# Matmuls that read the two halves of their moving operand by turns, in a two-layer transformer kernel

## The chip, the cores and the metric

The kernel runs on one NeuronCore of one Trainium2 chip, in a single launch. The metric is the device time of that core in microseconds (us), as the median of several runs. Engines are called as the profile calls them: PE (TensorE matmul), PEld (TensorE weight load), DVE (VectorE), ACT (ScalarE), POOL (GpSimd) and SP (SyncE, which issues the DMAs).

## The reference, cut to what matters

Sequence 1024, width 1024, two layers, all float32. Layer 0 mixes by sliding-window attention, layer 1 by a gated recurrence; both are followed by an MLP with a squared ReLU.

```python
for layer in range(DEPTH):                       # DEPTH = 2
    h = rmsnorm(x, mix_norm[layer])
    if layer % 2 == 0:
        y = sliding_window_attention(h, positions, attn_w_qkv[j], attn_b_qkv[j], attn_sinks[j], attn_w_o[j])
    else:
        y = hgrn2_recurrence(h, lbs[layer], hgrn_w_in[j], hgrn_g_norm[j], hgrn_w_o[j])
    x = x + y
    h = rmsnorm(x, mlp_norm[layer])
    x = x + jnp.square(jax.nn.relu(h @ mlp_w_up[layer])) @ mlp_w_down[layer]   # 1024 -> 4096 -> 1024
return rmsnorm(x, final_norm)
...
# attention: 16 query heads of 64 in 4 groups, each group with one key and value head;
# a query block of 128 sees its own and the previous block of keys, 256 in all
scores = jnp.einsum('bnqkgd,bnskd->bnkgqs', qb, kb) * (HEAD_DIM ** -0.5)
```

## The kernel before, in words

Activations lie with features on the 128 partitions and tokens along the free dimension, in two halves of 512 tokens (`TH`). So a product of a weight block and an activation is a matmul with the weights (128x128) stationary and the 512 tokens moving; in the query, key and value projection it is the other way round, 128 tokens stationary and 512 columns of weights moving. The result of each matmul fills one PSUM bank of 512 columns; there are four banks with tag `p` and four with tag `q`.

Float32 products are made from three matmuls in the format float32r. Each operand is split into a high part (a cast to float32r) and a low part (the rest); `mm3` multiplies high by high, high by low and low by high into the same bank. The splits are the bulk of the work on DVE and ACT: `weight_split` and `split` make a cast (on ACT or DVE) and a subtraction (DVE).

The large products use a two-by-two scheme with seven products in place of eight (Strassen's, in Winograd's order). `product` makes one of these: 4 blocks by 3 matmuls, 12 matmuls of 512 columns. The stages, in order of time, and their float32r matmuls of 512 columns:

- attention: the projection `qkv` (two halves, 3 column groups, 8 blocks, 4 token blocks, 3 matmuls: 576) and the output projection `o_proj` (2 by 8 by 8 by 3: 384), so 960. Between them, `attend_block` makes the scores of a query block: for four heads a matmul of 256 columns (the previous and the own block of 128 keys) with the keys' high part and one with their low part, 256 matmuls of 256 columns in all. The bank is then read in two parts: the own block's columns by a copy on ACT, the previous block's by a predicated copy on DVE.
- the MLP up projection `pair`: 16 pairs of row blocks, 7 products of 12 matmuls, 1344 in each layer. A product's bank is read by a copy on ACT or by an addition on DVE.
- the MLP down projection `down`: passes (1, 5), (6), (7), (4), (2), (3) over 16 blocks, each pass with 4 row blocks and 3 matmuls per product, 1344 in each layer. In the last layer, the last 96 of these are cut into 192 of half the width (256 columns: first tokens 0 to 255, then 256 to 511), so that the final norm and the stores of the first 256 tokens begin earlier: 1248 of 512 columns remain. `final` writes these with four DMAs for each half.
- the recurrence: `gates` and `two` make the projections of layer 1 (8 heads, 2 by 7 products, 12 matmuls: 1344), and `recurrence` the small float32 matmuls of the scan. In those, six levels of the scan use a moving operand of 32 columns out of a chunk of 64: at the first level every other column, at the last level 32 columns in a row.
- `hgrn_out`, the output projection of layer 1: 384.

Plain float32 matmuls (not float32r) remain in `spread` (512 columns), in the transposes (128 columns) and in the recurrence.

All operations are first recorded and then ordered by `Schedule.order`, a list scheduler: it plays the program with an estimated cost for every operation (the `cost` in `mm`, `act`, `copy`, `tt`, ...), fixed latencies between engines and a fixed number of buffers per tag, and issues each engine's instructions in the order that comes out. SP's queue holds the DMAs in that order too. Some operations may go to ACT or DVE (`ways`), and the scheduler chooses. So a changed cost in `mm` changes the order of all engines. Since every operation is recorded by one helper, the profile gives line 326 for nearly all of them, and groups are told apart by tile names: `a`, `t`, `m` are SBUF buffers, `wr` raw weights, `wh` and `wl` their high and low parts, `d` a buffer in DRAM.

Of the kernel before, what the change touches and what calls it, by code (L numbers as in the profile page):

```python
# [276 lines left out]

class Net:
# [153 lines left out]
    def sum_squares(self, tiles, n=TH):  # L432
        acc = None
        for x in tiles:
            sq = self.t()[:, :n]
            self.act(sq, x, AF.Square, n)
# [123 lines left out]

    def product(self, ps, w, x, start, n=TH):
# [19 lines left out]
    def pair(self, m, x):  # L581
# [3 lines left out]
        def read(ps):  # L585
            z = self.t()
            self.copy(z, ps)
            return z
# [13 lines left out]
        self.tt("DVE", u1, own, u1, ALU.add)  # L602
        self.square_relu(m, 0, u1, False)
        self.tt("DVE", u2, side, u2, ALU.add)
# [56 lines left out]
    def down(self, cut):  # L661
# [9 lines left out]
        def products(names, ps, ws, start, stop, tokens=slice(0, TH), ms=range(HK)):  # L671
            for p in ps:
                for name in names:
                    (wh, wl), (xh, xl) = ws[name, p]
                    for m in ms:
                        out = (main if name in (1, 6, 7, 4) else side)[m][:, tokens]
# [3 lines left out]
                        self.mm3(out, (wh[:, c], wl[:, c]), (xh[:, tokens], xl[:, tokens]), first, p == stop,  # L680
                                 tokens.stop - tokens.start, **more)
# [12 lines left out]
        def scaled_sum(hf, out, z, tokens=slice(0, TH)):  # L694

            k = tokens.stop - tokens.start
            u = self.t(tag="m")[:, :k]
            self.tt("DVE", u, z, self.r[hf][:, tokens], ALU.mult, k)
            part = out[:, tokens].only(tokens.start)
# [8 lines left out]
        for m in range(HK):  # L708
            y[0, 0, m], y[1, 1, m] = self.a(), self.a()
            self.copy(y[0, 0, m], main[m])  # L710
        for m in range(HK):
            self.copy(y[1, 1, m], side[m])
        run_pass((6,))
        for m in range(HK):
            u = y[0, 1, m] = self.a()
            self.copy(u, main[m])
# [4 lines left out]
        for m in range(HK):  # L721
            self.copy(parts[m], main[m])
# [14 lines left out]
        for m in range(HK):  # L737
            self.copy(parts[m], side[m])
# [17 lines left out]
        for c in (0, TH // 2):  # L756
            tokens = slice(c, c + TH // 2)
            for m in range(HK):
                products((3,), range(n - held, n), ws, False, n - 1, tokens, [m])
                scaled_sum(1, self.x[m][1], side[m][:, tokens], tokens)  # L760
            yield 1, tokens
# [100 lines left out]
    def keys_values(self, n, ps, r):  # L862
        W = NG * HD
        k = self.t(F32, (P, W))
        self.stt(k, ps[:, :W], r, self.bias[0][:, :W], ALU.mult, ALU.add, W)
# [3 lines left out]
        self.stt(v, ps[:, W:], r, self.bias[0][:, W:], ALU.mult, ALU.add, W)  # L869
# [61 lines left out]
    def attend_block(self, g, n, stacks):  # L931
# [7 lines left out]
        for h in range(4):  # L939
            self.mm(scores[h // 2][:, h % 2], stacks[h][:, tok], ks[:, c], h % 2 == 0, False, 2 * P)  # L940
        for h in range(4):
            self.mm(scores[h // 2][:, h % 2], stacks[h][:, tok], kl[:, c], False, h % 2 == 1, 2 * P)
# [29 lines left out]
    def o_proj(self, hf, out):  # L972

        a = [self.split(out[g, j]) for g in range(NG) for j in range(2)]
        for m in range(KT):
# [7 lines left out]
            self.tt("DVE", self.x[m][hf], ps, x, ALU.add)  # L983
# [62 lines left out]
    def two_first(self, which, e, x):  # L1046
# [6 lines left out]
        self.copy(y0, main)  # L1053
        self.product(own, w[1], x[2], True)
        self.tt("DVE", y0, own, y0, ALU.add)
        return main, y0

    def two(self, which, e, x, out, begun=None):
# [6 lines left out]
        if not begun:  # L1065
            self.product(main, w[1], x[1], True)
            self.copy(y0, main)
        yield
        self.product(side, w[5], x[5], True)
        self.copy(z1, side)  # L1070
        yield
        self.product(main, w[6], x[6], False)
        self.copy(y1, main)
        yield
        if not begun:
            self.product(own, w[2], x[2], True)
            self.tt("DVE", y0, own, y0, ALU.add)
        yield
        self.product(main, w[7], x[7], False)
        self.tt("DVE", z1, main, z1, ALU.add)  # L1080
        yield
        self.product(side, w[3], x[3], False)
        self.tt("DVE", y1, side, y1, ALU.add)
# [291 lines left out]
```

## Time and profile before

| what | value |
|---|---|
| median of 3 runs | 2181.03 us (2179.08 to 2183.65) |
| span of the profiled execution, first to last instruction | 2174.9 us |
| instructions | 32278 |
| PE busy | 2129.5 us (98%), 11374 matmul records |
| PEld busy | 1713.3 us (79%) |
| DVE busy | 1823.6 us (84%) |
| ACT busy | 837.7 us (39%) |
| POOL busy | 62.4 us (3%) |
| DMA | 316.49 MB, mean 146 GB/s, 44.7% of 16 engines' time |

The profile holds one execution, whose own time is known as its span alone: 2174.9 us, 6.1 us below the median of the runs. A matmul record lasts longer than the distance to the next one, since matmuls are pipelined; so the pace of the PE is read from start to start, or from a chain piece of many matmuls divided by their number. "Clock" is the share of full speed that the throttle granted.

### The profile page before, as it was taken

What the parts mean: (1) busy time and instruction counts of PE and PEld (TensorE: products, weight loads), DVE (VectorE), ACT (ScalarE), POOL (GpSimd) and SP (SyncE); (2) the same over time, 40 slices, a digit from 0 to 9 for tenths busy, and PEclk for the clock granted to TensorE, in tenths of its full rate; (3) what the DMA queues carried; (4) which work ended last, traced back from release to release, by engine and by line L of the source; (5) the groups of instructions that cost most, each with busy time, mean ns of one, the idle gap of its engine ahead of it and who ended that gap; (6) DMA issues with size and microseconds to landing.
All of it is one profiled execution on the core that took longest, in us unless ns stands there. A gap on an engine that the chain in (4) does not pass through costs nothing.

```text
span 2174.9 us, 32278 instructions
## 1 busy us (share of the span) xinstructions
PE 2129.5 (98%) x11374; PEld 1713.3 (79%) x11374; DVE 1823.6 (84%) x3608; ACT 837.7 (39%) x1757; POOL 62.4 (3%) x124
## 2 busy tenths in 40 slices
PE   8999999999999999999999999999999999999997
PEld 6777778888877887877788888878788887888786
DVE  8899889667789888899888888878976678988887
ACT  5567755122234233365333333343521223322442
POOL 4030000000000000000100000000000000000000
PEclk9999999999999999999999999999999999999999
DMA  6212363333369867741111111547333336976652
GB/s 204 75 48 83 112 194 116 105 109 111 108 204 305 274 202 234 247 136 49 56 57 59 58 53 52 188 148 227 113 114 103 107 116 224 305 241 226 209 171 78
DMA packets 174274, 316.49 MB, mean 146 GB/s; under 512 B 19616, under 2 KB 21664, under 8 KB 174112
## 3 DMA queue, kind: packets, MB, share of 16 engines
q1 hardware_dynamic: 174112, 314.43, 44.7%
q8 instruction: 89, 1.46, 0.3%
q14 instruction: 73, 0.60, 0.1%
HBM read 250.39 MB, written 63.96 MB: 145 GB/s over the span
## 4 chain that ended last, share of the span: by engine, by line
PE 85%; DVE 7%; ACT 4%; DMA 2%; issue 1%; SPq 0%; DVEq 0%; ACTq 0%
PE q L326 45%; PE p L326 40%; DVE a L326 3%; DVE t L326 2%; ACT t L326 1%; ACT a L326 1%; DVE wl L326 1%; DVE m L326 1%; DMA wr<-in_down 1%; ACT m L326 1%; ACT wh L326 0%; DMA t<-d 0%; DVE wh L326 0%; DMA d<-t 0%; DMA a<-d 0%
## 5 line engine op out<-in xcount | busy, mean ns | idle before, releaser
L326 PE MATMUL q<-a,wh 128*128 128x512 f32 x2560 | 798.6, 395 | 5.0 <-DVE t L326 2.3
L326 PE MATMUL p<-a,wh 128*128 128x512 f32 x2336 | 754.4, 402 | 9.1 <-ACT t L326 3.7
L326 PEld LDWEIGHTS q<-a,wh 128*128 128x128 f32 x2560 | 480.1, 188 | 120.5 <-ACT t L326 4.1
L326 PEld LDWEIGHTS p<-a,wh 128*128 128x128 f32 x2336 | 432.0, 189 | 107.7 <-ACT t L326 4.6
L326 PE MATMUL q<-a,wl 128*128 128x512 f32 x1280 | 499.5, 394 | 0.0
L326 PE MATMUL p<-a,wl 128*128 128x512 f32 x1168 | 462.8, 397 | 0.0
L326 PEld LDWEIGHTS q<-a,wl 128*128 128x128 f32 x1280 | 240.4, 188 | 56.6
L326 PEld LDWEIGHTS p<-a,wl 128*128 128x128 f32 x1168 | 220.4, 189 | 50.5 <-issue 0.5
L326 DVE TENSOR_TENSOR wl<-wr,wh 128x512 fp32r<-128x512 f32 x352 | 241.0, 686 | 15.5 <-ACT wh L326 5.4
L326 ACT COPY t<-q 128x512 f32<-128x512 f32 (+2 forms) x201 | 111.8, 562 | 349.0 <-PE q L326 344.1
L326 DVE TENSOR_TENSOR a<-t,a 128x512 fp32r<-128x512 f32 (+1 forms) x294 | 195.0, 685 | 0.8 <-DMA t<-d 0.5
L326 DVE CAST wh<-wr 128x512 fp32r<-128x512 f32 x204 | 87.8, 430 | 127.6 <-PE p L326 78.4
L326 DVE TENSOR_TENSOR wl<-m,wh 128x512 fp32r<-128x512 f32 x256 | 176.3, 689 | 16.1 <-ACT wh L326 6.1
L326 ACT CAST wh<-m 128x512 fp32r<-128x512 f32 x153 | 95.2, 623 | 210.4 <-PE q L326 148.4
L326 DVE TENSOR_TENSOR t<-t,t 128x512 f32<-128x512 f32 (+3 forms) x268 | 159.7, 611 | 17.7 <-DMA t<-d 10.7
L326 ACT CAST a<-t 128x512 fp32r<-128x512 f32 x189 | 114.7, 619 | 128.8 <-PE q L326 82.6
L326 ACT CAST wh<-wr 128x512 fp32r<-128x512 f32 x148 | 91.1, 619 | 172.7 <-PE p L326 109.3
L326 PE MATMUL p<-wh,a 128*128 128x512 f32 x384 | 130.6, 407 | 8.2 <-ACT a L326 7.0
L326 DVE TENSOR_TENSOR m<-wr,wr 128x512 f32<-128x512 f32 x160 | 109.7, 687 | 22.2 <-DMA wr<-in_down 11.9
L326 PEld LDWEIGHTS q<-t,t 128*64 128x64 f32 (+1 forms) x2160 | 98.0, 144 | 25.0 <-issue 11.2
L326 PE MATMUL q<-t,t 128*64 128x32 f32 (+2 forms) x2160 | 111.5, 230 | 0.0
L326 DVE CAST wh<-m 128x512 fp32r<-128x512 f32 x103 | 44.3, 430 | 73.4 <-PE q L326 59.7
(117 smaller groups left out, 2113.9 us busy)
## 6 DMA issues: line engine op xcount, KB each, us to landing
t<-d SPq DMA_DIRECT2D x296, 256.0 KB, 4.7
wr<-in_down SPq DMA_DIRECT2D x256, 256.0 KB, 3.9
d<-t SPq DMA_DIRECT2D x180, 256.0 KB, 2.4
wr<-in_up SPq DMA_DIRECT2D x128, 256.0 KB, 2.9
wr<-in_win SPq DMA_DIRECT2D x68, 256.0 KB, 2.9
a<-d SPq DMA_DIRECT2D x60, 256.0 KB, 4.4
wr<-in_wqkv SPq DMA_DIRECT2D x48, 256.0 KB, 2.8
d<-a SPq DMA_DIRECT2D x48, 256.0 KB, 2.4
```

The costliest lines, as they stand in the source:

```text
L326: fn(*[place(a) for a in args], **{k: place(v) for k, v in kw.items()})
```

## The change

In `mm3`, the moving operand of 512 columns is read through a view that goes to and fro between its two halves: column 0, column 256, column 1, column 257, and so on (`turned`). In the cut end of the last layer, a matmul of 256 columns reads 128 columns of the first half and 128 of the second by turns. The score matmuls do the same with 256 columns of keys: previous block and own block by turns. Stationary operands are as before, and the matmul still writes its bank in one run.

The bank therefore holds its columns in the turned order, and everything that reads such a bank takes every other column of it twice: the first half of the result lies in the even columns, the second half in the odd ones (`straight`, written to or combined with the two halves of an ordinary tile, `halves`). No instruction is added for this: copies on ACT and additions and multiplications on DVE get views of three dimensions in place of two. The query's bias sum, the key and value sums and the two reads of the scores are changed in the same way.

The cut end is cut otherwise: the first piece is tokens 0 to 127 and 256 to 383, the second the rest. `final` works on views of two runs of 128 columns, and writes each of its pairs with two DMAs in place of one, of 128 KB each in place of 256 KB: 16 stores in place of 8 there.

The scheduler's cost of a matmul becomes n * rate / 2.4 + 3 ns for all; before it was n / 2.25 + 4 for those with rate 1 (231.6 ns for 512 columns, now 216.3) and n * rate / 2.4 + 4 for the rest. So the order of all engines is made anew from other costs.

```diff
+def turned(z):
+    return z.rearrange("p (a b) -> p b a", a=2)
+
+def straight(z):
+    return z.rearrange("p (b a) -> p a b", a=2)
+
+def halves(z):
+    return z.rearrange("p (a b) -> p a b", a=2)
...
     def mm(self, out, lhsT, rhs, start, stop, n=TH, rate=1.0, form="whole", late=(), **kw):
-        cost = n * rate / (2.25 if rate == 1.0 else 2.4) + 4
+        cost = n * rate / 2.4 + 3
...
-    def mm3(self, out, w, x, start, stop, n=TH, **kw):
+    def mm3(self, out, w, x, start, stop, n=TH, cols=slice(0, TH), **kw):
         (wh, wl), (xh, xl) = w, x
+        xh, xl = (turned(z)[:, cols.start // 2 : cols.stop // 2] for z in (xh, xl))
         self.mm(out, wh, xh, start, False, n, **kw)
...
+    def take(self, out, bank):
+        self.copy(halves(out), straight(bank))
+
+    def add_bank(self, z, bank, to=None):
+        self.tt("DVE", halves(z if to is None else to), straight(bank), halves(z), ALU.add)
...
         if psum:
-            self.act(r, c, AF.Relu)
-            self.stt(r, c, 0.0, r, ALU.max, ALU.mult)
+            c, h = straight(c), halves(r)
+            self.act(h, c, AF.Relu)
+            self.stt(h, c, 0.0, h, ALU.max, ALU.mult)
...
-            self.copy(z, ps)
+            self.take(z, ps)
...
-        self.tt("DVE", u1, own, u1, ALU.add)
+        self.add_bank(u1, own)
...
-            self.stt(q, ps, r, self.bias[cg], ALU.mult, ALU.add)
+            self.stt(halves(q), straight(ps), r, halves(self.bias[cg]), ALU.mult, ALU.add)
...
         for h in range(4):
-            self.mm(scores[h // 2][:, h % 2], stacks[h][:, tok], ks[:, c], h % 2 == 0, False, 2 * P)
+            self.mm(scores[h // 2][:, h % 2], stacks[h][:, tok], turned(ks[:, c]), h % 2 == 0, False, 2 * P)
...
-            self.copy(mj, ps[:, :, P:], 2 * P)
-            prev = ps[:, :, :P] if n else self.neg.unsqueeze(2).to_broadcast([P, 2, P])
+            ps = ps.rearrange("p h (s a) -> p h a s", a=2)
+            self.copy(mj, ps[:, :, 1], 2 * P)
+            prev = ps[:, :, 0] if n else self.neg.unsqueeze(2).to_broadcast([P, 2, P])
...
-            self.dma(self.io["out"][hf, k : k + per, :, tokens].rearrange("k p t -> p k t"), pair, 4 * P * TH)
+            to = self.io["out"][hf, k : k + per].rearrange("k p t -> p k t")
+            if n == TH:
+                self.dma(to, pair, 4 * P * TH)
+                continue
+            for a in range(2):
+                c, h = a * TH // 2, slice(a * n // 2, (a + 1) * n // 2)
+                self.dma(to[:, :, c + piece.start : c + piece.stop], pair[:, :, h], 2 * P * TH)
```

More of the change, by code (lines that the diff above doesn't have):

```diff
@@ L692, in run_pass, with scaled_sum @@
             return ws
[L694 to L699, printed above, removed]
+        def scaled_sum(hf, out, z, cols=slice(0, TH)):
+            k, piece = cols.stop - cols.start, slice(cols.start // 2, cols.stop // 2)
+            u = halves(self.t(tag="m")[:, :k])
+            z = straight(z[:, cols]) if z.buf.tag in "pq" else halves(z)
+            self.tt("DVE", u, z, halves(self.r[hf])[:, :, piece], ALU.mult, k)
+            part = halves(out)[:, :, piece].only(cols.start)
             self.tt("any", part, u, part, ALU.add, k)
@@ L721, in down @@
         for m in range(HK):
-            self.copy(parts[m], main[m])
+            self.take(parts[m], main[m])
         for m in range(HK):
@@ L737, in down @@
         for m in range(HK):
-            self.copy(parts[m], side[m])
+            self.take(parts[m], side[m])
         for m in range(HK):
@@ L1052, in two_first @@
         self.product(main, w[0], x[1], True)
-        self.copy(y0, main)
+        self.take(y0, main)
         self.product(own, w[1], x[2], True)
-        self.tt("DVE", y0, own, y0, ALU.add)
+        self.add_bank(y0, own)
         return main, y0
@@ L1076, in two @@
             self.product(own, w[2], x[2], True)
[L1077 removed]
+            self.add_bank(y0, own)
         yield
         self.product(main, w[7], x[7], False)
[L1080 removed]
+        self.add_bank(z1, main)
         yield
         self.product(side, w[3], x[3], False)
[L1083 removed]
+        self.add_bank(y1, side)
         yield
         self.product(main, w[4], x[4], False)
[L1086 removed]
+        self.take(z0, main)
         yield
@@ L1263, in hgrn, with final @@
         self.hgrn_out(1, ys[1], totals[1])
-    def final(self, hf, tokens=slice(0, TH)):
-        n = tokens.stop - tokens.start
-        xs = [self.x[kt][hf][:, tokens].only(tokens.start) for kt in range(KT)]
+    def final(self, hf, cols=slice(0, TH)):
+        n, piece = cols.stop - cols.start, slice(cols.start // 2, cols.stop // 2)
+        xs = [halves(self.x[kt][hf])[:, :, piece].only(cols.start) for kt in range(KT)]
+        if n == TH:
+            xs = [z.rearrange("p a b -> p (a b)") for z in xs]
+        same = (lambda z: z) if n == TH else halves
         r, rs = self.rstd(self.sum_squares(xs, n), n=n), self.t()[:, :n]
```

51 lines of the change are left out of this document (25 added, 26 removed).

## The prediction

> **What bounds the kernel now.** I read the page's first and fourth parts first, then the chain of waits in order of time, then busy time by stretches, then the groups of matmuls.
>
> ```profile
> PE 2129.5 (98%) x11374; PEld 1713.3 (79%) x11374; DVE 1823.6 (84%) x3608; ACT 837.7 (39%) x1757; POOL 62.4 (3%) x124
> PE 85%; DVE 7%; ACT 4%; DMA 2%; issue 1%; SPq 0%; DVEq 0%; ACTq 0%
> 442.06 16.67 PE q L326 x72
> 461.51 16.70 PE q L326 x72
> 400.00:600.00 200.00, 200.00 (x865) 162.08 (x864) 142.54 (x245) 41.02 (x72) 0.00 (x0) 1.00 0.33 107
> 760.00:860.00 100.00, 99.71 (x431) 80.47 (x430) 87.75 (x151) 36.22 (x63) 0.00 (x0) 1.00 0.67 219
> ```
>
> PE holds 85% of the chain that ended last. DVE is busy for 84% of the span, so it stands close behind. The third and fourth lines are pieces of the chain, start and length: 72 matmuls of 512 columns in 16.70 us, 231.9 ns each, with no wait among them. The last two are stretches of plain matmuls (length, then busy time of PE, PEld, DVE, ACT, POOL with counts, granted clock, DMA share, GB/s): 200 us for some 864 and 100 us for some 430, so 231.5 and 232.6 ns. The clock is 1.00 in both, while DVE goes from 71% to 88%, ACT from 21% to 36% and the DMA engines from 0.33 to 0.67. The pace does not follow them, so it belongs to PE itself.
>
> **The change, part by part.** First the pace. These rows tell what makes 231.9:
>
> ```profile
> 216.84 2.39 PE L326 MATMUL q<-t,a 128*128 128x256 f32 x19
> 2139.00 1.02 PE L326 MATMUL q<-t,c 128*128 128x512 f32 x2
> L326 PE MATMUL q<-t,c 128*128 128x512 f32 x18 | 9.0, 597 | 0.3 <-DVE t L326 0.3
> 1064.23 0.60 PE L326 MATMUL q<-c,t 128*128 128x128 f32 x4
> L326 PE MATMUL q<-c,t 128*128 128x128 f32 x136 | 21.7, 275 | 1.1 <-ACT t L326 0.7 <-DVE t L326 0.5
> L326 PE MATMUL q<-a,a 128*128 128x256 f32 x128 | 28.4, 305 | 3.9 <-DVE a L326 1.5 <-DVE t L326 1.0 <-DVE m L326 0.6
> ```
>
> The first row is 19 score matmuls of 256 columns in float32r; less about 0.29 us for the last one's own length, that is 2.10/18 = 117 ns each. From 117 at 256 and 231.9 at 512, a column takes 0.449 ns and a matmul 2 ns besides. The excess is thus paid per column and not per weight load, which is 128 columns in both. The next rows are plain float32: the second 512-wide record starts 1.02 - 0.597 = 0.42 us after the first, and the 128-wide ones follow each other at (0.60 - 0.275)/3 = 0.108 us. That is 0.82 ns a column, and half of it is 0.41. I take plain float32 to go over each column twice, since its pace is nearly half of that of float32r; then the array can take a column in 0.41 ns where it is not held up, and float32r, at 0.449, is held up for about 8% of its time. What differs is how fast it asks for new columns, and that is what the turned read changes.
>
> So the price of a turned matmul lies between two ends. The lower is 512 x 0.41 + 2, some 213 ns. The upper is the plain float32 record, 425 ns, if every column must be fetched anew because its neighbour in time is 1 KB away. Between them the rows nearest to a stepped moving read are the levels of the recurrence:
>
> ```profile
> 1028.91 1.12 PE L326 MATMUL q<-t,t 128*64 128x32 f32 x32
> 1053.45 1.12 PE L326 MATMUL q<-t,t 128*64 128x32 f32 x32
> ```
>
> These are the first level (every other column) and the last (32 columns in a row) of one head, of six alike: 32 matmuls take 1.12 us in both, so a step of two costs nothing there. That form asks for columns at half the pace, and its step is 8 bytes and not 1 KB, so it does not exclude a loss; but it shows that the moving read needs no run. I take 216.5 ns: near the lower end, with 3 ns for what the rounding of the rows leaves open. That saves 15.4 ns on each full-width matmul and half of it on each of 256 columns.
>
> [...]
>
> Now how many, and where they lie on the path. The counts of float32r matmuls are 960 in attention, 1344 each in the two up projections, the first down projection and the gates, 384 in the recurrence's output projection, 1248 in the last down projection. Their sum, 7968, is that of the groups:
>
> ```profile
> L326 PE MATMUL q<-a,wh 128*128 128x512 f32 x2560 | 798.6, 395 | 5.0 <-DVE t L326 2.3 <-ACT t L326 1.8 <-ACT wh L326 0.9
> L326 PE MATMUL p<-a,wh 128*128 128x512 f32 x2336 | 754.4, 402 | 9.1 <-ACT t L326 3.7 <-ACT wh L326 3.2 <-DVE t L326 1.4
> L326 PE MATMUL q<-a,wl 128*128 128x512 f32 x1280 | 499.5, 394 | 0.0
> L326 PE MATMUL p<-a,wl 128*128 128x512 f32 x1168 | 462.8, 397 | 0.0
> L326 PE MATMUL p<-wh,a 128*128 128x512 f32 x384 | 130.6, 407 | 8.2 <-ACT a L326 7.0 <-ACT wh L326 1.2
> L326 PE MATMUL p<-wl,a 128*128 128x512 f32 x192 | 77.3, 403 | 0.0
> L326 PE MATMUL p<-a,a 128*128 128x512 f32 x48 | 11.4, 395 | 0.0
> ```
>
> The full saving is 7968 x 15.4 = 122.7 us, and 448 x 7.7 = 3.4 us for the narrow ones. Not all of it reaches the end, since DVE, ACT and DMA end some waits. I weigh each stage by PE's share of the chain in it. Busy time by stage (attention, up, down, gates, last down), then the chain of attention, up, down, gates and output projection:
>
> ```profile
> 0.00:340.00 340.00, 323.14 (x1698) 252.16 (x1699) 301.12 (x698) 212.44 (x599) 46.89 (x98) 0.99 0.38 120
> 340.00:655.00 315.00, 314.96 (x1359) 254.41 (x1359) 238.22 (x412) 82.25 (x147) 0.00 (x0) 1.00 0.39 127
> 655.00:965.00 310.00, 305.67 (x1310) 246.81 (x1309) 270.92 (x491) 121.55 (x212) 0.36 (x2) 0.99 0.73 238
> 965.00:1450.00 485.00, 479.29 (x3869) 386.51 (x3869) 422.30 (x950) 185.25 (x378) 9.70 (x18) 1.00 0.24 75
> 1845.00:2140.00 295.00, 292.81 (x1279) 236.98 (x1278) 256.92 (x443) 109.34 (x194) 0.00 (x0) 1.00 0.66 216
> by line: PE p L326 51.4%; PE q L326 18.6%; ACT a L326 5.9%; ACT t L326 4.2%; DVE t L326 3.9%; ACT m L326 3.9%; DVE a L326 3.0%; issue 2.2%; DVE wl L326 1.7%; DVE m L326 1.5%; DMA a<-in_x 1.2%; ACT wh L326 0.8%; DVE wh L326 0.5%; ACT L326 0.
> by line: PE q L326 80.1%; PE p L326 13.2%; DVE a L326 2.4%; DVE wl L326 1.2%; DMA t<-d 1.1%; DVE t L326 1.1%; issue 0.5%; DVE m L326 0.2%; DVE wh L326 0.1%; SPq L326 0.1%; DVEq L326 0.0%
> by line: PE q L326 40.0%; PE p L326 34.9%; DVE a L326 9.0%; DMA wr<-in_down 3.3%; DVE wl L326 2.9%; issue 2.6%; DVE m L326 2.4%; DMA a<-d 1.3%; DMA t<-d 1.1%; DVE wh L326 0.7%; ACT wh L326 0.5%; ACT a L326 0.4%; ACT t L326 0.4%; SPq L326 0.
> by line: PE p L326 67.1%; PE q L326 23.7%; DVE t L326 2.5%; ACT t L326 1.8%; DVE m L326 1.4%; issue 1.2%; ACT a L326 0.7%; ACT wh L326 0.4%; DVE wl L326 0.4%; DVE a L326 0.3%; ACT L326 0.3%; DVE wh L326 0.2%; ACT m L326 0.1%; DVEq L326 0.0%
> by line: PE p L326 62.1%; DVE a L326 9.1%; DVE t L326 8.0%; DVE wl L326 5.4%; ACT t L326 3.6%; PE q L326 3.4%; DMA wr<-in_wg 3.1%; issue 3.1%; DVE m L326 1.3%; ACT a L326 0.6%; DVE wh L326 0.5%; DVE sm L326 0.1%
> ```
>
> - attention: 14.8 us x 0.70 = 10.3
> - first up projection: 20.7 x 0.93 = 19.3
> - first down: 20.7 x 0.75 = 15.5
> - gates: 20.7 x 0.91 = 18.8
> - output projection: 5.9 x 0.655 = 3.9
> - second up, with the first one's share: 19.3
> - last down: DVE is at 87%, as in the first, so I take a share between that one's 0.75 and the up projection's 0.93: 19.2 x 0.85 = 16.3
> - narrow matmuls, at attention's share: 3.4 x 0.70 = 2.4
>
> Together 105.8 us. DVE's share rises by this, from 84% to 1823.6/2069 = 88%, and in the first down projection from 87% to 270.9/294.5 = 92%; what is late next there is DVE's subtractions for the splits, and the weights' transfers (DMA share 0.73, then 0.77). That is why I do not take the whole 126.
>
> The readers of the banks. Each now takes every other column of PSUM. The trace has no such read, so its cost is bounded:
>
> ```profile
> L326 ACT COPY t<-q 128x512 f32<-128x512 f32 x175 | 102.2, 586 | 338.9 <-PE q L326 338.3 <-DVE a L326 0.5
> L326 DVE TENSOR_TENSOR t<-p,t 128x512 f32<-128x512 f32 x96 | 65.4, 683 | 1.2 <-PE p L326 1.1
> L326 DVE TENSOR_TENSOR t<-t,m x192: 407/419/460, 1033.9 to 1439.5; 128x256 f32<-128x256 f32 x192
> L326 DVE TENSOR_TENSOR t<-q,t 128x512 f32<-128x512 f32 x32 | 21.9, 684 | 0.1
> ```
>
> The third row is the recurrence's multiplications on halves of chunks, runs of 1 to 64 columns: 407 to 460 ns whatever the run, so stepping costs DVE nothing in SBUF. That is the nearest row, and I take nothing for PSUM. The other end is a doubled read. A column costs DVE (683 - 419)/256 = 1.03 ns, so 530 ns more on each of some 204 full reads and 265 on 80 half reads (up 96, gates 48, the projections 48, down 12; keys, values, scores and the cut end): 129 us of DVE. On ACT some 264 copies would grow by at most their own 586 ns, but those wait 338 us for PE as it is.
>
> The new order. The scheduler now believes in 216.3 ns, close to the 216.5 that I expect, so its due times stay about as true as before; transfers and splits are placed earlier against PE's queue by the same share. I take nothing, with 10 us to either side. The waits change no engine's work.
>
> The end. There SP issues more stores:
>
> ```profile
> L326 SPq DMA_DIRECT2D out<-a x16: 332/377/1538, 2140.8 to 2171.1; - x16
> ```
>
> Eight more issues of 0.33 us; only the last pair's extra one lies behind all work: 0.3 us later, at most 1.5. I add 0.5.
>
> The sum is 2174.9 - 105.8 + 0.5 = 2069.6 for the span, and with the 6.1 us by which the median exceeds it 2075.7. I predict 2076 us, with an own range of 2045 (213 ns, nearly all on the path) to 2110 (DVE holds a further third).
>
> **The rivals.** First, the one on the other side: the moving read fetches a stretch of neighbouring columns at once and uses all of it when it goes in order; turned, every fetch serves one column. Its place is every one of the 7968 matmuls. For it speaks that the present read is already held up at 0.449 ns a column, so something on that path is short; against it, that a step of two costs nothing in the rows above. It decides as soon as a matmul takes over 231.9 ns. At plain float32's pace, 425, it costs 7968 x 193 = 1540 us: some 3720 us. If it only doubles the present excess, it is 247 ns, +106 us: 2287. I give this 0.13. [...]
>
> Second, the banks' readers. If a stepped read of PSUM is doubled on DVE, 25 us of the 129 fall on the gates (448 of then 466 us) and over 30 on attention, where DVE is at 301 of 340 us, which takes their savings and more. The up projection hides its 25 us: of 315 us DVE leaves 77 idle, of which the saving takes 19. The gain then falls by some 45 us: 2120. For it: no row shows such a read; against: the SBUF row. Chance 0.08.
>
> Third, the turned read changes nothing, because the limit is not in which columns follow each other: 231.9 stays, and the time is 2181 + 0.5, with a few us for an order planned on too short a cost. Chance 0.05.
>
> **How the numbers follow.** The likeliest case has 0.74. To hold 8 in 10, the range takes the second rival in: 2045 to 2135. A difference of 0.2%, 4.4 us, is about what a measurement of this kernel tells from none. Faster is 0.74 + 0.08 and 0.01 of the third; the same 0.03; slower 0.13 and 0.01 of the third.
>
> **What would show it.** The chain's pieces of 72 matmuls should last 15.6 us in place of 16.70, and the up projection's stretch 295 us in place of 315. The rows of `t<-q` on ACT and `t<-p,t` on DVE should stay at 586 and 683 ns. PE's share of the chain should fall in the down projections and DVE's busy time stay at 1824 us. I am wrong in the pace if pieces of 72 last 16.7 us or more; in the weighing, if they are short and the stages do not follow.

## The result, and the profile after

The changed kernel takes 2077.41 us (median of 4 runs, 2076.22 to 2080.61); the kernel before took 2180.06 us beside it (4 runs). The ratio is 0.953, with a 95% interval of 0.9516 to 0.9543. The profiled execution has a span of 2074.4 us against 2174.9 us: 100.5 us less.

The first fence has the page's busy times and the chain by engine; the second the first pieces of the chain through the up projection (start, length, engine, number of matmuls). The third has the two stretches of plain matmuls: length, busy time and count of PE, PEld, DVE, ACT and POOL, then granted clock, DMA share and GB/s.

```profile
PE 2009.9 (97%) x11374; PEld 1722.8 (83%) x11374; DVE 1809.3 (87%) x3598; ACT 841.8 (41%) x1767; POOL 63.8 (3%) x124
...
PE 77%; DVE 14%; DMA 3%; ACT 3%; issue 2%; SPq 0%; DVEq 0%; ACTq 0%
```

```profile
348.15 15.54 PE q L341 x72
366.28 15.54 PE q L341 x72
```

```profile
400.00:600.00 200.00, 200.00 (x924) 174.41 (x923) 153.83 (x274) 39.20 (x69) 0.00 (x0) 1.00 0.39 124
760.00:860.00 100.00, 99.80 (x462) 86.83 (x461) 85.51 (x146) 36.99 (x65) 0.00 (x0) 1.00 0.81 264
```

Pieces of 72 matmuls last 15.54 us: 215.8 ns each, where it was 231.9. The 200 us of the first stretch hold 924 matmuls in place of 865. DVE's busy time is nearly what it was (1823.6 before), so its share rose with the shorter span, and its share of the chain doubled, from 7% to 14%. PE's share of the chain fell from 85% to 77%.

The readers of the banks, by the groups of instructions (count, then busy us and mean ns):

```profile
L341 ACT COPY t<-q 128x512 f32<-128x512 f32 x175 | 101.9, 585 | 308.2 <-PE q L341 307.1 <-DVE a L341 1.0
L341 DVE TENSOR_TENSOR t<-p,t 128x512 f32<-128x512 f32 x96 | 65.3, 683 | 2.6 <-PE p L341 1.8 <-ACT t L341 0.7
```

585 and 683 ns, against 586 and 683: in these groups, reading every other column of PSUM costs neither engine anything.

The stages in us, between landmarks that both traces have (the first matmul of a pair, of a pass or of a head's scan). Two more kernels, told below, stand beside them. The forecast is the prediction's term for the stage, divided evenly over its pairs or heads where a landmark cuts it:

| stage | before | new costs alone | turned alone | both (the change) | saved | forecast |
|---|---|---|---|---|---|---|
| attention, first pair of up | 364.0 | 361.8 | 360.4 | 348.0 | 16.0 | 13.9 |
| first up, 14 pairs | 274.3 | 274.5 | 255.5 | 255.5 | 18.8 | 16.9 |
| last pair, passes (1, 5) of down | 103.9 | 103.0 | 100.7 | 99.7 | 4.2 | |
| passes 6, 7, 4 | 134.0 | 133.4 | 133.4 | 125.0 | 9.0 | |
| passes 2, 3, first head's gates | 149.0 | 148.2 | 146.5 | 141.8 | 7.2 | 19.1 for these three |
| gates, 6 heads | 334.7 | 336.6 | 321.3 | 323.0 | 11.7 | 14.1 |
| last gates, output projection, first pair | 194.4 | 200.7 | 193.7 | 193.7 | 0.7 | 7.5 |
| second up, 14 pairs | 274.0 | 274.1 | 255.5 | 255.5 | 18.5 | 16.9 |
| last down and the end | 346.4 | 345.6 | 343.3 | 332.3 | 14.1 | 17.0 |

The saving by PE's own account: 7968 matmuls at 231.8 - 215.9 ns are 126.7 us and the 448 narrow ones (118 to 111 ns) some 2.9, 129.6 together. Against them stand 19.6 us more of waits and slower matmuls among the wide ones, 7.3 on the other PE work and 2.3 before the first and after the last of them. The traces name the places: in the changed kernel PE waits at seven places for 1.9 to 10.1 us, and then the clock is 0.5 for 3.4 to 14.6 us. Two such places of the changed kernel, around 927 and 1390, in the columns of the stretches:

```profile
915.00:927.00 12.00, 8.89 (x42) 7.44 (x40) 12.00 (x21) 8.88 (x17) 0.00 (x0) 0.98 0.06 22
927.00:941.00 14.00, 6.97 (x17) 5.25 (x18) 14.00 (x27) 6.79 (x13) 0.00 (x0) 0.53 0.26 75
1387.00:1394.00 7.00, 5.62 (x13) 4.53 (x14) 5.46 (x11) 3.85 (x7) 0.00 (x0) 0.53 0.41 152
```

Around 927 the first down projection hands its sums to the norm and the gates' splits: DVE is busy without a gap for 26 us, PE is not, and PE's clock goes to 0.53. All stretches at half clock together are 26.9 us in the trace before and 52.1 us in this one. The waits of PE grew in the same way, before and then after (the columns: us in total, times, longest):

```profile
PE p L326 <- ACT wh L326: 4.4, 2, 3.2
...
PE q L326 <- ACT t L326: 2.5, 6, 0.7
```

```profile
PE q L341 <- DVE t L341: 13.8, 9, 4.9
PE p L341 <- ACT wh L341: 13.0, 3, 10.1
PE q L341 <- ACT t L341: 8.7, 12, 3.0
```

### The profile page after: what moved, and what is told of

It is laid out like the page before. It is cut to its first block, busy times and chain, and to the rows that moved or that the text cites. A ratio compares the mean times of both kernels' runs of the same rounds, so it can differ in the third digit from the quotient of the medians.

```text
span 2074.4 us, 32285 instructions
## 1 busy us (share of the span) xinstructions
PE 2009.9 (97%) x11374; PEld 1722.8 (83%) x11374; DVE 1809.3 (87%) x3598; ACT 841.8 (41%) x1767; POOL 63.8 (3%) x124
## 4 chain that ended last, share of the span: by engine, by line
PE 77%; DVE 14%; DMA 3%; ACT 3%; issue 2%; SPq 0%; DVEq 0%; ACTq 0%
PE q L341 44%; PE p L341 33%; DVE a L341 6%; DVE t L341 4%; DVE m L341 2%; DVE wl L341 2%; DMA wr<-in_down 2%; ACT t L341 1%; ACT a L341 1%; DMA a<-in_x 0%; DMA t<-d 0%; DVE sm L341 0%; DMA t<-in_x 0%; DMA a<-d 0%; ACT wh L341 0%
## 5 line engine op out<-in xcount | busy, mean ns | idle before, releaser
L341 PE MATMUL q<-a,wh 128*128 128x512 f32 x2560 | 763.1, 381 | 10.1 <-ACT t L341 5.9
L341 PE MATMUL p<-a,wh 128*128 128x512 f32 x2336 | 721.4, 388 | 12.9 <-ACT wh L341 11.2
L341 PEld LDWEIGHTS q<-a,wh 128*128 128x128 f32 x2560 | 485.5, 190 | 83.8 <-ACT t L341 8.3
L341 PE MATMUL q<-a,wl 128*128 128x512 f32 x1280 | 483.1, 381 | 0.3 <-DVE wl L341 0.3
L341 PE MATMUL p<-a,wl 128*128 128x512 f32 x1168 | 447.8, 384 | 0.0
L341 DVE TENSOR_TENSOR wl<-m,wh 128x512 fp32r<-128x512 f32 x256 | 175.0, 685 | 8.2 <-ACT wh L341 1.3
L341 ACT CAST a<-t 128x512 fp32r<-128x512 f32 x198 | 119.5, 617 | 118.7 <-PE q L341 47.5
L341 ACT CAST wh<-m 128x512 fp32r<-128x512 f32 x145 | 89.7, 620 | 144.1 <-PE q L341 80.8
L341 PE MATMUL p<-wh,a 128*128 128x512 f32 x384 | 121.8, 389 | 10.1 <-ACT a L341 8.3
L341 ACT CAST a<-a 128x512 fp32r<-128x512 f32 x111 | 67.7, 620 | 79.5 <-DVE a L341 39.5
```

Source lines behind the costliest of these rows:

```text
L341: fn(*[place(a) for a in args], **{k: place(v) for k, v in kw.items()})
```

## The experiments

### Each half of the change by itself

The first kernel is the one before with the new cost, the second the changed one with the old cost:

```diff
 # e1_order: the kernel before
-        cost = n * rate / (2.25 if rate == 1.0 else 2.4) + 4
+        cost = n * rate / 2.4 + 3
 # e2_pace: the changed kernel
-        cost = n * rate / 2.4 + 3
+        cost = n * rate / (2.25 if rate == 1.0 else 2.4) + 4
```

> The kernel before with one edit: the scheduler's new cost of a matmul (n * rate / 2.4 + 3 ns), every operand read in order as before. Theory (the pace of the turned read makes the gain): the chain's pieces of 72 matmuls stay at 16.70 us, and the time stays within 0.4% of before, 2172 to 2189 us. Rival (part of the gain is the new order): the pieces stay, but waits shrink and the time falls by 0.5 to 1.5%, 2148 to 2170 us. A second question: the recurrence's multiplications at the first level (DVE t<-t,t of 128x256 in the gates' stretch) took 411 to 471 ns before and 475 to 602 after. If the order makes that, they are over 500 ns here; if the turned read does, they stay at 411 to 471.

> The changed kernel with the scheduler's old cost (n / 2.25 + 4 ns where the rate is 1), every operand read by turns. Theory: pieces of 72 matmuls last 15.5 us, 215.6 ns each, and the time is that of the changed kernel within 0.4%, ratio to before 0.949 to 0.957. Rival (the order does part): the ratio lies halfway or nearer to 1, 0.96 to 0.99. The multiplications at the first level are over 500 ns by the account that the turned read slows them, and under 471 by the account that the order does.

The new costs alone: 2178.3 us, ratio 0.9989 (0.9981 to 0.9998), some 2 us. The turned operand alone: 2110.33 us, ratio 0.9674 (0.9659 to 0.9689), some 70 us. Together they bring 102.7. The first result is as the theory had it, the second is the rival's. So the costs are worth 2 us where the matmul takes 231.8 ns and some 30 us where it takes 215.9 (2110.33 against 2077.41, and 2081.07 in a repeat): they pay only when they are true. The table of stages shows where. The up projections have 255.5 us whatever the costs. In attention, in the passes 6, 7, 4 and in the last down projection the turned operand alone gains 3.6, 0.6 and 3.1 us, with both 16.0, 9.0 and 14.1. The passes 6, 7, 4 in the trace with old costs, the stretch and PE's waits in it, and then both with new ones:

```profile
717.00:850.00 133.00, 126.73 (x576) 109.22 (x575) 116.93 (x203) 43.79 (x76) 0.00 (x0) 0.97 0.70 228
```

```profile
PE q L341 <- ACT t L341: 5.8, 1, 5.8
```

```profile
703.00:828.00 125.00, 124.80 (x577) 108.70 (x576) 113.61 (x198) 46.96 (x82) 0.00 (x0) 1.00 0.77 251
```

```profile
PE q L341 <- ACT t L341: 0.2, 1, 0.2
```

The same 576 matmuls: with the old costs PE waits 5.8 us for one copy on ACT, and the clock is 0.97 over the stretch (6.8 us at half) where it is 1.00. That accounts for the 8 us between these two traces, but not for a gain of the costs. A repeat of the changed kernel (`a1_after`, told in the last part of this section) takes 128.9 us for this stage, with the same wait:

```profile
PE q L341 <- ACT t L341: 2.9, 1, 2.9
```

And a kernel with the new costs and turns between neighbouring blocks (`n1_near16`) waits 4.7 us there and takes 133.4. So the length of this wait changes from one execution to another, and a stage of one trace is known to some 4 us only. That the costs gain some 30 us in all is shown by the medians; by which waits they do it stays open.

### Which orders of reading are fast

A kernel, run once, that gives each pair of the up projections and each head of the gates its own order of the moving columns. The readers of the banks stay as in the change, so its columns come out in other orders.

```diff
+def every(s):
+    return lambda z: z.rearrange("p (a b) -> p b a", b=s)
+def near(d):
+    return lambda z: z.rearrange("p (o a b) -> p o b a", a=2, b=d)
+def runs(c):
+    return lambda z: z.rearrange("p (a b c) -> p b a c", a=2, c=c)
...
-            xh, xl = (turned(z)[:, cols.start // 2 : cols.stop // 2] for z in (xh, xl))
+            xh, xl = view(xh), view(xl)
```

`every(s)` takes every s-th column, then the rest (512/s places in turn); `near(d)` goes to and fro between neighbouring blocks of d columns; `runs(c)` goes to and fro between the halves in runs of c.

> The changed kernel, with other views of the moving operand in the 32 pairs of the up projections (one view for all 84 matmuls of a pair) and in the gates (one view for each of the 8 heads); the banks are read as in the changed kernel, so that the columns of the results lie in another order there. Views: a step of s (columns 0, s, 2s, ..., then 1, s+1, ...) with s of 1, 2, 4, ..., 256, of which 1 is the order of before and 256 is the change; turns between neighbouring blocks of d columns, d of 2 to 128; turns between the two halves in runs of c columns, c of 2 to 64. Theory A (two places at least some distance apart must take turns): 231 to 233 ns a matmul for s of 1 and small s, 215 to 216 from some distance on, both in the steps and in the blocks. Theory B (any order in which neighbours in time are not neighbours in place): 215 to 216 for s of 2 already, and for all d; runs of 2 and more fall back to 224 or above. [...]

The chain of this kernel through the first up projection: start, length and count. Each piece is one product of 12 matmuls, all in one order. Their orders, one after the other: every 2nd, 4th, 8th, 16th, 32nd, 64th, 128th and 256th column, then neighbouring blocks of 2 and of 4:

```profile
369.18 5.43 PE p L361 x12
...
407.30 5.53 PE p L361 x12
...
445.68 5.18 PE p L361 x12
...
481.98 5.21 PE p L361 x12
...
518.45 5.22 PE p L361 x12
...
555.62 5.81 PE p L361 x12
...
594.00 3.36 PE p L361 x12
...
616.71 2.59 PE p L361 x12
...
635.05 2.78 PE p L361 x12
...
654.34 2.59 PE p L361 x12
```

And from the second layer, to and fro between the halves in runs of 4 and of 64, blocks of 128 by turns, and columns in order:

```profile
1740.04 2.96 PE p L361 x12
...
1821.46 2.79 PE p L361 x12
...
1840.76 2.59 PE p L361 x12
1859.08 2.77 PE p L361 x12
```

Divided by 12, in ns for a matmul of 512 columns:

| order | ns |
|---|---|
| in order | 231 |
| every 2nd, 4th, 8th, 16th, 32nd, 64th column | 453, 461, 432, 434, 435, 484 |
| every 128th: four places in turn | 280 |
| every 256th: two places, 1 KB apart (the change) | 216 |
| blocks of 2 by turns: two places, 8 bytes apart | 232 |
| blocks of 4 by turns: two places, 16 bytes apart | 216 |
| blocks of 8 to 128 by turns | 216 |
| halves by turns, in runs of 4 and of 64 | 247, 232 |
| halves by turns, in runs of 2, 8, 16 and 32 (from the starts of the matmuls) | 328, 243, 241, 236 |

So the gain has a narrow condition: of these orders, only two places by turns, one column from each, 16 bytes to 1 KB apart, took 216 ns. Two places 8 bytes apart were as slow as reading in order (232 and 231 ns). Four places in turn were slower than in order (280), so were 8 places and more (432 to 484), and a step of 2 is among the worst (453). Neither theory on record covers all of these; what makes an order fast is not shown.

### Taking work off DVE

If the missing part of the 129.6 us lies behind DVE, it should come out when DVE has less to do. First the weights' low parts are left out, in the changed kernel and in the one before alike (the high part is used in their place, so that the number of matmuls stays); then the activations' low parts too:

```diff
 # e4_light_turned (changed kernel), e5_light_plain (kernel before): weights
-        hi, lo = (self.tile(tag, BUFS[tag], (P, TH), F32R) for tag in ("wh", "wl"))
+        hi = self.tile("wh", BUFS["wh"], (P, TH), F32R)
...
-        self.tt("any", lo, z, hi.bitcast(F32), ALU.subtract)
-        return hi, lo
+        return hi, hi
 # e6_bare_turned, e7_bare_plain: the same, and in the activations' split
-        hi, lo = ((new or self.a)(F32R) for _ in range(2))
+        hi = (new or self.a)(F32R)
...
-        self.tt("any", lo, src, hi.bitcast(F32), ALU.subtract)
-        return hi, lo
+        return hi, hi
```

> The changed kernel without the low parts of the weights that pass through weight_split: the subtraction on DVE is left out, and the third matmul of each three reads the high part again. That takes some 660 subtractions of 0.686 us, 450 us, from DVE. Theory (what the change did not gain was held by DVE): DVE is at some 66%, PE's waits shrink, and the time is 125 to 132 us below that of the same kernel read in order. Rival (the missing part was lost elsewhere, in latencies or in a slower reading of the banks): the difference stays near the 100 us that the full kernels show, 95 to 110.

> The kernel before with the same subtractions left out, read in order: the partner of the run with turned reads. Pieces of 72 matmuls at 16.70 us; the time falls below the kernel before by the waits of PE, some 40 to 60 us of 2175, to 2115 to 2140 us. Theory (DVE held the rest): 125 to 132 us above its partner; rival: 95 to 110 above.

Without the weights' low parts: 2060.36 us turned and 2166.56 us plain, ratios to the kernel before of 0.9444 (0.9427 to 0.9461) and 0.9937 (0.992 to 0.9954). The difference is 106 us, near the 102.7 of the full kernels and in the rival's range, with DVE's busy time down by 331 and 341 us. The plain kernel had been expected at 2115 to 2140 us; it won only 14 us, so DVE's load held it back little. DVE's total load is therefore not what holds the missing 27 us back; where the splits of the activations follow each other, DVE was still full (40.4 us of 45 from 1430 on in the turned kernel). That led to the second pair.

> The changed kernel without the low parts of weights and activations: the subtractions of both kinds of split are left out, and every three matmuls read the high parts three times. With the weights' low parts alone left out, the difference between turned and plain was 106 us, and in the stretch of the second up projection's start DVE was still at 90% (40.4 of 45 us), with the activations' splits. Theory (at the handovers between stages DVE's chain of activation splits sets the end, so a faster PE only arrives earlier): now the difference to the partner is 118 to 130 us, and the stretch from the last heads of the recurrence to the second up projection, which saved 0.7 us of some 10, saves 6 or more. Rival (a latency that is not DVE's work, or the cost of the halved clock): 100 to 112 us, and that stretch still saves under 3.

> Its partner: the kernel before with the same subtractions left out, read in order. Theory: 118 to 130 us above its partner; rival: 100 to 112.

Without the activations' low parts as well: 2047.49 us turned (2040.03 to 2052.98) and 2165.87 us plain (2161.59 to 2167.23), ratios 0.9394 (0.937 to 0.9419) and 0.9925 (0.9906 to 0.9945). The difference is 118.4 us in the medians and 125.0 in the profiled spans, at the low edge of what the theory gave and 12 and 20 more than with the weights alone. The stretch from the last gates to the second up projection shows it, first in the kernel before, then in the changed kernel, the bare turned one and the bare plain one:

```profile
1360.00:1554.00 194.00, 189.66 (x1274) 152.66 (x1274) 165.88 (x361) 78.93 (x149) 1.18 (x4) 1.00 0.53 172
```

```profile
1293.00:1487.00 194.00, 185.77 (x1277) 157.99 (x1277) 166.42 (x359) 79.58 (x150) 1.34 (x4) 0.96 0.53 172
```

```profile
1272.00:1455.00 183.00, 178.83 (x1270) 153.78 (x1266) 125.83 (x284) 74.65 (x140) 1.39 (x4) 1.00 0.49 156
```

```profile
1348.00:1543.00 195.00, 191.94 (x1252) 154.69 (x1251) 125.69 (x283) 72.82 (x136) 1.23 (x4) 0.99 0.45 143
```

DVE has the same 166 us of 194 before and after, and the turned read saves 0.7 us here (194.4 to 193.7). With DVE at 126 us of 183 it saves 11.8 (194.6 to 182.8 between the landmarks, a pair of 19.6 added to the plain kernel's 175.0 since its landmark lies one pair earlier), the whole of what 384 + 168 + 84 matmuls at 15.9 ns can bring, 10.1, and a little of the clock. The plain kernel does not get faster there with the lighter DVE, so it was bound by PE. The changed kernel is bound at the handover by what the bare one leaves out: DVE's subtractions, the waits behind them and the half clock after these (13.7 us of this stretch in the changed kernel, none in the bare turned one). Leaving out the low parts also frees their buffers; no run separates that from DVE's time.

### Is it the half clock, or DVE?

With the waits of PE in the changed kernel the clock goes to 0.5: 13.7 us of it at 927, 6.8 each at 1387 and 1466. If the slow matmuls that follow cost time of their own, matmuls without use that fill the wait should win some of it; if DVE sets the end of the stretch anyway, nothing is won. The fillers are matmuls of 128 columns on a constant, laid at the norms after a down projection:

```diff
+    def warm(self, times, *late):
+        lead, self.s.lead = self.s.lead, -3000
+        for _ in range(times):
+            ps = self.psum("q")
+            for k in range(4):
+                self.mm(ps[:, k * P : k * P + P], self.warm_w, self.warm_w, True, True, P, 1.0, "whole", late)
+        self.s.lead = lead
...
+            self.warm(20, self.x[KT - 1][1])     # w1_warm: 20, 20, 40; w2_warm, n2_near_warm: 5, 7, 20
```

A second kernel goes with these, in which the turns are between neighbouring blocks of 16 columns (64 bytes) and not between the halves; the cut end and its stores are as in the kernel before. It tests a side effect that the trace after shows: DVE's multiplications in the recurrence became slower (418 to 540 ns at the first level). Its expectation says lines for places at least 16 bytes apart: two of these by turns took 216 ns above. A third is the changed kernel again, as it is.

```diff
 # n1_near16; the projection of queries and keys and the scores stay as in the change
+NEAR = 16
 def turned(z):
-    return z.rearrange("p (a b) -> p b a", a=2)
+    return z.rearrange("p (o a b) -> p o b a", a=2, b=NEAR)
```

> The changed kernel unchanged, on the same chip as the next two: 0.951 to 0.955 of before.

> The changed kernel with the turns between neighbouring blocks of 16 columns (64 bytes apart) in place of the halves (1 KB apart) in all products but the query, key and value projection and the scores; the cut end and its stores as in the kernel before. Theory (any two lines by turns lift the stall; the 1 KB distance is what slows DVE's stepped operations): pieces of 72 matmuls at 15.5 us; the recurrence's multiplications at the first level back at 400 to 475 ns from 475 to 602; the gates' six periods 2 to 5 us shorter than the 323.0 of the changed kernel; the time 2 to 10 us below it. Rival (DVE is slowed by any turned read): multiplications over 500 ns and the same time within 0.2%. Readers of banks: copies on ACT stay at 586 ns and additions on DVE at 683 if stepped reads in runs of 16 cost nothing too.

> The changed kernel with 320 added matmuls of 128 columns on constants, whose results nobody reads, in three waits of PE: between the first down projection and the gates (160), before the recurrence's output projection (80) and before the second up projection (80). In the changed kernel's trace, these waits are followed by 13.7, 6.8 and 6.8 us at a granted clock of 0.5. Theory (the waits cost twice, by themselves and by the halved clock after them): the stretches at 0.5 go, matmuls there are at 216 and not 427 ns, and the time falls by 5 to 14 us below the changed kernel (half of 27 us at most). Rival (DVE sets the end there whatever the clock): the stretches go, and the time stays within 0.2%.

> As the run with 320 added matmuls, with 128 of them (80, 28 and 20 at the three places): there they took 0.112 us each and 36.4 us in all against waits of some 10, 3.8 and 2.7 us, so that the filling itself cost more than the waits; now 9.0, 3.1 and 2.2 us. Theory (a wait costs once by itself and once more by the halved clock): no stretch at a clock of 0.5 after the three places, and 4 to 13 us below the changed kernel, ratio to before 0.947 to 0.952 (the changed kernel has 0.953 to 0.954). Rival (DVE sets the end): the stretches go, and the ratio stays at 0.953 to 0.954.

> The kernel with turns between blocks of 16 columns (ratio 0.9522) with the same 128 added matmuls. If both edits act by themselves, the ratio is 0.945 to 0.950, the best of all versions; if the clock does not matter, 0.952.

| kernel | median, us | ratio to the kernel before |
|---|---|---|
| changed kernel again | 2081.07 | 0.9539 (0.9525 to 0.9552) |
| near blocks | 2074.78 | 0.9522 (0.9504 to 0.9540) |
| changed, 320 fillers | 2098.80 | 0.9616 (0.9601 to 0.9632) |
| changed, 128 fillers | 2083.31 | 0.9538 (0.9517 to 0.9560) |
| near blocks, 128 fillers | 2082.76 | 0.9547 (0.9528 to 0.9565) |

The 320 fillers overshoot: 160 of them take 18 us where the wait was some 10, so that kernel loses time to them and decides nothing. Of the 128, 80 lie at the first place (927), 28 at the second (1390) and 20 at a third (1466, 6.8 us at half clock in the changed kernel). The first two places in the kernel with 128:

```profile
915.00:930.00 15.00, 15.00 (x71) 13.15 (x70) 14.99 (x26) 9.83 (x18) 0.00 (x0) 1.00 0.20 74
930.00:945.00 15.00, 13.28 (x99) 12.31 (x99) 15.00 (x27) 9.93 (x19) 0.00 (x0) 1.00 0.21 60
1385.00:1402.00 17.00, 13.65 (x66) 10.79 (x65) 11.69 (x34) 6.63 (x12) 0.00 (x0) 0.70 0.40 133
```

The clock stays at 1.00 around 930, and DVE is busy for 29.99 of 30 us as before. The time of the kernel is the same (0.9538 against 0.9539), but that does not decide, since several differences add up in it. The starts of the same matmuls in the two traces separate them: how far the kernel with 128 fillers lies behind the changed kernel, in us.

| place | before the wait | first matmuls behind it | after the half clock |
|---|---|---|---|
| first | 6.3 | 6.3 | 3.8 |
| second (half clock in both) | 3.8 | 7.9 | 7.0 |
| third | 7.0 | 7.2 | 4.8 |

At the first place the wait ends at the same time with fillers or without: DVE's splits and the casts on ACT end it. Behind it the changed kernel has 14 matmuls at half clock, some 427 ns each, where the other has 216, and the 2.5 us that this brings are still there at the second place, 430 us later. At the third place it is 2.4 us, and the kernel of near blocks shows the same there with fillers. At the second place the clock stays at half (0.70 over the third line above) and the fillers cost 3.2 us. So the half clock is a cost beside the wait, about 2.5 us at each of the two places. In the sum it does not show: the second place takes most of it back, the 6.3 us were there before the first filler, and the last down projection, without fillers, is 4.8 us longer in this trace. The kernel of near blocks with fillers, expected at 0.945 to 0.950 or at 0.952, has 0.9547, so both expectations failed.

For DVE, the groups of the recurrence's multiplications, before, after and with near blocks. The first level, which takes every other column, is 32 of the 46 in the second line of each; the first line has the other six levels, on runs of 2 to 64 columns, 32 each:

```profile
L326 DVE TENSOR_TENSOR t<-t,m 128x256 f32<-128x256 f32 x192 | 68.6, 420 | 1.1 <-PE q L326 1.1
L326 DVE TENSOR_TENSOR t<-t,t 128x256 f32<-128x256 f32 x46 | 17.6, 427 | 1.8 <-ACT t L326 1.4
```

```profile
L341 DVE TENSOR_TENSOR t<-t,m 128x256 f32<-128x256 f32 x192 | 71.1, 436 | 1.2 <-PE q L341 1.2
L341 DVE TENSOR_TENSOR t<-t,t 128x256 f32<-128x256 f32 x46 | 21.2, 521 | 1.7 <-ACT t L341 1.4
```

```profile
L357 DVE TENSOR_TENSOR t<-t,m 128x256 f32<-128x256 f32 x192 | 68.5, 419 | 1.2 <-PE q L357 1.2
L357 DVE TENSOR_TENSOR t<-t,t 128x256 f32<-128x256 f32 x46 | 18.1, 438 | 1.7 <-ACT t L357 1.4
```

Two levels make the difference: the first went from a median of 418 ns to 540 with the halves and is at 421 with near blocks, and the one on runs of 2 went from 420 to 536 and is at 418. The other five stay at 416 to 419. With the new costs alone the first level has 418 ns, with the turned operand alone 526, so the order of the work does not make it. Near blocks have the same pace of PE (216 ns), so the pace does not make it either; the distance between PE's two places matters. It is not all: in the one run of the many orders, the first level has 504 ns beside runs of 4 from the two halves, but 432 and 416 beside runs of 2 and of 8 (medians of four each), though these are 1 KB apart too. What else it takes stays open. The slowing is not on the path: the six heads take 322.9 us with near blocks and 323.0 with halves, and the two kernels' intervals overlap, with medians 6.3 us apart. No version was shown to be faster than the changed kernel.

## Why the prediction was right, point by point

- **The pace.** Forecast 216.5 ns, measured 215.8 to 216, between the ends 213 and 425. Of the argument, that PE is held up by how fast it gets columns and that the order of reading changes this, the second part is shown: the order alone moves the pace from 216 to 484 ns. The first remains the author's reading. That this order is one of the fast ones was luck. The low end leaned on the recurrence's rows, where a step of 2 seemed to cost nothing. A row of the same head, of 32 matmuls with twice as many columns, all in a row, shows that these rows could not tell:

```profile
1025.30 1.15 PE L326 MATMUL q<-t,t 128*64 128x64 f32 x32
```

They take 1.15 us with 64 columns and 1.12 with 32, so their columns do not set their pace, and a column at twice the price would not have shown. In float32r a step of 2 takes 453 ns. So the trace before held nothing against the first rival, and every order with four places or more (280 to 484 ns) would have borne it out. That plain float32 goes over each column twice, from which the lower end comes, is not shown by any run.
- **The readers of the banks** at nothing: right, 585 and 683 ns. The rival that doubles them fell. The row named as nearest holds runs of 2 to 64 columns; the multiplications on every other column are in another group (`t<-t,t`, 410 to 471 ns before), and the change slowed them, which the prediction did not foresee and which cost nothing on the path.
- **The new order** at nothing, 10 us to either side: here the prediction's step was mis-sized. The costs are worth 2 us without the new pace and some 30 with it. It did not show in the sum, presumably since the weighing already took an order as good as the one before and the new costs provide it. Had the change come without them, 2110 us would have been the time, at the edge of the likeliest case's own range.
- **The weighing by PE's share of the chain**: 105.8 us forecast for 100.5 measured in the spans. The sum is right, its parts less so, and part of its closeness is luck: misses of either sign cancel. Up projections: 1.33 us a pair against 1.21, the whole of the pace, as they have no other bound. Attention: 16.0 against 13.9. Gates: 1.95 us a head against 2.35, though PE held 91% of their chain. Gates' end, output projection and first pair: 0.7 against 7.5, the largest miss; a share of the chain tells what was bound before, and here DVE's splits, 166 of 194 us already before, and the half clock behind the waits for them took the rest. The half clock is in no term of the sum. The prediction named these subtractions as what is late next, but in the first down projection, which kept its saving.
- **DVE's busy time** at 1824 us: 1809.3. PE's share of the chain fell, as forecast.
- **The end**: the rows of the two traces that start the last sum, before and after:

```profile
2166.55 1.22 PE L326 MATMUL q<-t,c 128*128 128x256 f32 x2 [2.00 <-DVE t L326]
```

```profile
2065.12 1.22 PE L341 MATMUL q<-t,c 128*128 128x256 f32 x2 [2.07 <-DVE t L341]
```

From there to the end of the span are 8.4 us before and 9.3 after: 0.9 us more, where 0.5 was taken, between 0.3 and 1.5.

## What to carry to other kernels

When an engine that bounds the kernel goes at a steady pace without waits, ask in which order it reads; here the access pattern alone took a matmul from 231.9 to 215.8 ns. But try the exact pattern, since other orders took up to 484 ns. When a planner orders the work, give it the new cost together with the new pace: here some 30 of the 103 us hung on that. And a saving on the bounding engine ends where the next engine has no gap left, so before weighing by shares of the chain, look at each handover between stages for the work that PE will wait for next. The busy share alone does not tell: DVE was at 87% in the first down projection, which kept its saving, and at 86% in the stretch from the last gates to the second up projection, which lost it. And count a wait of PE with the half clock behind it, here some 2.5 us at each of two places.

## What the runs showed of the hardware that was not expected

- A float32r matmul of 512 columns took 216 ns with one column by turns from each of two places 16 bytes to 1 KB apart, 232 with 8 bytes between the places, 231 in order, 280 with four places, 432 to 484 with 8 places or more.
- While PE read single columns from two places 1 KB apart by turns, DVE's multiplications in SBUF on every other column, and on runs of 2, were slower (medians of 418 and 420 ns before, 540 and 536 after); with 64 bytes between the places they were not (421 and 418). Those on runs of 4 to 64 columns kept their time (416 to 419 ns).
- In the traces before and after, the granted clock went to 0.5 at twelve places, 1.2 to 4.8 us after the start of a PE wait of 1.5 to 10.1 us. It stayed there for 3.4, 6.8 or 13.7 us, at the last place to the end of the span (9.9 and 14.6 us). A matmul of 512 columns then took 427 ns. Two other waits, of 1.55 and 1.76 us (at 84 and 15 in the trace after), had a clock of 1.00 behind them. At two places where fillers kept the clock at 1.00, some 2.5 us each were won behind the wait.
- 32 plain float32 matmuls with 64 stationary columns took 1.12 us with 32 moving columns and 1.15 us with 64.
